# Two joins of a two-layer trunk on one core: when a norm's sums, its weights and the columns of a last step come

## The chip, the cores and the metric

The kernel runs on one core of a Trainium2 chip. The metric is the device time of one execution in microseconds; the time of a kernel is the median over its runs. TensorE (PE) multiplies, VectorE (DVE), ScalarE (ACT) and GpSimd (POOL) do elementwise work, SyncE (SP) issues the loads. TensorE's clock has two levels, 2.4 and 1.2 GHz; the profile shows the granted one as a share of the full one.

## The reference

Two layers over 512 latent columns and 256 context columns, each of 1024 features in float32. Layer 0 mixes with an mLSTM, layer 1 with windowed attention to latent and context keys; each is followed by an MLP.

```python
def _rms_norm(x, g):
    xf = x.astype(F32)
    y = xf * lax.rsqrt(jnp.mean(xf * xf, axis=-1, keepdims=True) + NORM_EPS)
    return (y * g.astype(F32)).astype(x.dtype)
...
def _modulate(x, shift, scale):
    return x * (1.0 + scale) + shift
...
def _sq_relu_mlp(u, w1, w2):
    return jnp.square(jax.nn.relu(u @ w1)) @ w2
```

Every mixer and every MLP reads `_modulate(_rms_norm(h), shift, scale)` and adds its result, times a gate, to `h`. What follows is about two places: from layer 0's output projection to its MLP, and from that MLP's last step to the keys of layer 1.

## The kernel before, in words

Features lie on partitions, in 8 tiles of 128 (index m or kt); columns lie along the free axis, latent (L, 512) and context (C, 256) apart. A float32 product is three matmuls (`mm3`, L96 to L98): high part times high, high times low, low times high. So every weight is split: `unit` loads a block of 512 KB (a DMA on SP into one of three raw buffers), ACT casts the high part (whi, L919), DVE subtracts to get the low one (wlo, L920), into one of four pairs of buffers. The order of instructions on each engine is made by a scheduler when the program is built, from the order of the code and from the buffers; it is fixed at run time. `feed` takes the next unit of a list, the plan, and puts it on the list `begun`; with `feed(True)` its cast and subtraction keep their place in the program.

A norm needs, for every column, the sum of squares over 8 tiles. `norm_add` (L302, L306) squares a tile on ACT and adds it to the tile ssC or ssL, on POOL; with `apart` the last two squares are not added but kept as tiles of their own (sq). Squares have two buffers, so one waits until the square two before it is used up. `norm_rc` then sums over partitions on TensorE: for every block of 128 columns one matmul against a column of ones for each kept tile (L319), below called ones-matmuls. DVE makes rs from it (L322), POOL raises it to the power -1/2 (rc, L324), TensorE turns rc into rows (L332, four transposes for L, two for C). Then DVE, ACT and DVE make u for each tile: t = h times both factors (L962 in the MLP, L341 in layer 1), the high part uH (or uC), and the low part uL.

**Join 1** is `out_late`. Products of heads 0 to 5 for the tiles 6 and 7 come first: (6,L), (6,C), (7,L), (7,C), 18 matmuls each. Then, for C and after it for L, each of the eight tiles gets the part of heads 6 and 7 (`wl`), DVE adds it to h (L508), and `norm_add` follows. `norm_hooks` gives two steps: the sums (`norm_rc`) and the whole norm. The C hooks run after the first two L tiles, the L hooks in `plain`, the MLP's first chunk, behind the C products of its tiles 0 and 1. `plain` takes four units of w1, C columns first.

```python
for g in "CL":
    for n, m in enumerate((6, 7, 0, 1, 2, 3, 4, 5)):
...
        self.norm_add(self.st, g, n, self.out_add(m, g, t), apart=n > 5)
```

**Join 2** is the last chunk (c = 7) of `ffn0` and `keys_begin`. There the columns are in two halves of 384: t = 0 is latent 0 to 383, t = 1 is latent 384 to 511 with all of C. `back` multiplies the hidden tiles (12 matmuls for each tile m and half) with units of w2 and adds to h (L1156). Tiles 0 to 3 are done for both halves, unit after unit, then tiles 4 to 7 for t = 1 and for t = 0. The C hooks run at tiles 4 and 5 of t = 0. `keys_begin` loads the four key units (wskv) and multiplies them with the context columns (96 matmuls, pj), with the L hooks after the first and the second half of the first block; the latent keys follow in `layer1_mix`, and their results go through rp, ksp and ks to the transposes of L1489.

## Time and profile before

| what | value |
|---|---|
| median of 3 runs (lowest, highest) | 1603.83 us (1600.60, 1606.53) |
| the profiled execution, its span | 1609.09 us, 1607.3 us |
| mean granted clock | 0.986 |
| PE, weight load of PE | 1552.3 us (97%), 1390.9 us (87%) |
| DVE, ACT, POOL | 1007.7 us (63%), 677.1 us (42%), 404.1 us (25%) |

The profile is one execution; its times count from the start of the span. Rows of a timeline give the start, the length, the engine, the line and operation, out<-in, the shape and how often, and in brackets the idle time just before and what ended it. A matmul's length covers its passage through the engine, so the distance of two starts tells what one costs; a ones-matmul is two records. A window's row gives its length and the busy time of PE, PE's weight load, DVE, ACT and POOL (with how many instructions), then the granted clock, the DMA engines' busy share and GB/s.

### The profile page before, as it was taken

The page shows a single profiled execution, that of the slowest core. Times are in us where ns is not written, and L with a number is a line of the kernel's source. Part 1 is how long each engine was busy: PE and PEld are TensorE (multiplying, and loading weights), DVE is VectorE, ACT ScalarE, POOL GpSimd, SP SyncE. Part 2 cuts the span into 40 slices and gives each one's busy share as a digit, 9 for nine tenths or more (in the row PEclk, how much of TensorE's full clock was granted, in tenths as well). Part 3 has the DMA queues.
Part 4 walks back from the last instruction along what each step waited for, and adds up shares of the span by engine and source line. Part 5 has one row for each costly group of instructions (what it writes and reads, how often), then busy time and mean ns, then how long its engine had stood idle before and what let it go on. Part 6 is the DMA issues. An engine that isn't in the chain of part 4 may idle for free.

```text
span 1607.3 us, 23962 instructions
## 1 busy us (share of the span) xinstructions
PE 1552.3 (97%) x9246; PEld 1390.9 (87%) x9246; DVE 1007.7 (63%) x1886; ACT 677.1 (42%) x1399; POOL 404.1 (25%) x378
## 2 busy tenths in 40 slices
PE   7989999999999999999999999989999999999997
PEld 4768888878899999999999998888887888888886
DVE  3665647478586888777667666767887533333333
ACT  4433333344473432433524445666675423233231
POOL 0221111113303221322232230454443302011122
PEclk9999999999999999999999999999999999999999
DMA  8322323134221343344344321010111322332221
GB/s 304 135 72 100 118 68 109 66 115 152 85 79 40 117 136 128 119 150 147 113 142 132 118 79 34 27 51 16 54 40 36 110 92 92 97 100 92 92 92 53
DMA packets 48857, 156.77 MB, mean 98 GB/s; under 512 B 5439, under 2 KB 11071, under 8 KB 48615
## 3 DMA queue, kind: packets, MB, share of 16 engines
q1 hardware_dynamic: 46992, 153.73, 29.2%
q8 instruction: 73, 1.20, 0.3%
q10 hardware_dynamic: 1751, 1.51, 0.3%
q14 instruction: 41, 0.34, 0.1%
HBM read 153.12 MB, written 2.10 MB: 97 GB/s over the span
## 4 chain that ended last, share of the span: by engine, by line
PE 72%; DVE 7%; issue 5%; POOL 5%; ACT 5%; DMA 1%; POOLq 0%; DVEq 0%; ACTq 0%
PE mm L97 17%; PE mm L96 17%; PE mm L98 17%; DVE adap L273 2%; PE p L97 2%; PE p L98 2%; PE p L96 2%; PE pt L1580 1%; PE pj L96 1%; PE pj L97 1%; PE pj L98 1%; PE at L836 1%; ACT whi L919 1%; DVE wlo L920 1%; PE av L1596 1%
## 5 line engine op out<-in xcount | busy, mean ns | idle before, releaser
L919 ACT CAST whi<-raw 128x1024 fp32r<-128x1024 f32 (+2 forms) x183 | 183.8, 1009 | 255.2 <-PE mm L97 208.7
L920 DVE TENSOR_TENSOR wlo<-raw,whi 128x1024 fp32r<-128x1024 f32 (+2 forms) x180 | 216.3, 1206 | 114.2 <-ACT whi L919 109.3
L96 PE MATMUL mm<-uH,whi 128*128 128x512 f32 (+1 forms) x488 | 188.8, 392 | 4.1 <-ACT v L702 4.0
L97 PE MATMUL mm<-uL,whi 128*128 128x512 f32 (+1 forms) x488 | 186.2, 384 | 0.3
L98 PE MATMUL mm<-uH,wlo 128*128 128x512 f32 (+1 forms) x488 | 185.4, 383 | 0.0
L273 DVE SCALAR_TENSOR_TENSOR adap<-raw,crow 128x1024 bf16<-128x1024 f32 x128 | 166.2, 1299 | 21.6 <-DMA raw<-ada 20.8
L96 PE MATMUL mm<-h,whi 128*128 128x384 f32 x512 | 173.2, 338 | 1.8 <-ACT h L919 1.8
L97 PE MATMUL mm<-h,whi 128*128 128x384 f32 x512 | 172.5, 337 | 0.5 <-DVE h L920 0.3
L98 PE MATMUL mm<-h,wlo 128*128 128x384 f32 x512 | 172.1, 336 | 0.0
L894 POOL TENSOR_TENSOR r<-r 128x512 f32<-128x512 f32 (+1 forms) x35 | 52.2, 1493 | 259.8 <-ACT r L893 259.8
L96 PEld LDWEIGHTS mm<-uH,whi 128*128 128x128 f32 x488 | 91.8, 190 | 20.5 <-ACT v L702 4.2
L97 PEld LDWEIGHTS mm<-uL,whi 128*128 128x128 f32 x488 | 92.2, 190 | 17.6 <-issue 1.2
L98 PEld LDWEIGHTS mm<-uH,wlo 128*128 128x128 f32 x488 | 91.9, 189 | 17.9 <-issue 0.3
L96 PE MATMUL mm<-hH,whi 128*128 128x512 f32 (+1 forms) x272 | 104.0, 382 | 0.0
L97 PE MATMUL mm<-hL,whi 128*128 128x512 f32 (+1 forms) x272 | 103.9, 382 | 0.0
L98 PE MATMUL mm<-hH,wlo 128*128 128x512 f32 (+1 forms) x272 | 103.8, 382 | 0.0
L919 ACT CAST whi<-sum 128x512 fp32r<-128x512 f32 (+1 forms) x42 | 31.9, 762 | 168.2 <-PE mm L97 77.8
L96 PEld LDWEIGHTS mm<-h,whi 128*128 128x128 f32 x512 | 96.1, 188 | 2.7 <-ACT h L919 2.7
L97 PEld LDWEIGHTS mm<-h,whi 128*128 128x128 f32 x512 | 96.2, 188 | 1.3 <-DVE h L920 1.2
L98 PEld LDWEIGHTS mm<-h,wlo 128*128 128x128 f32 x512 | 96.1, 188 | 0.0
L904 DVE SCALAR_TENSOR_TENSOR hL<-mm,mod,hL 128x512 f32<-128x512 f32 (+1 forms) x34 | 24.5, 720 | 102.7 <-PE mm L98 102.7
L98 PE MATMUL p<-t,wlo 128*128 128x384 f32 x224 | 75.4, 337 | 0.4 <-DVE wlo L920 0.4
(354 smaller groups left out, 4003.4 us busy)
## 6 DMA issues: line engine op xcount, KB each, us to landing
raw<-w SPq DMA_DIRECT2D x96, 512.0 KB, 3.4
raw<-ada SPq DMA_DIRECT2D x80, 512.0 KB, 3.5
raw<-w2a SPq DMA_DIRECT2D x32, 512.0 KB, 3.5
adaw<-ada SPq DMA_DIRECT2D x16, 512.0 KB, 6.8
hL<-xT SPq DMA_DIRECT2D x16, 256.0 KB, 4.1
raw<-wqk SPq DMA_DIRECT2D x8, 512.0 KB, 3.9
raw<-wv SPq DMA_DIRECT2D x8, 512.0 KB, 3.6
raw<-wo SPq DMA_DIRECT2D x8, 512.0 KB, 3.4
```

Source lines behind the costliest of these rows:

```text
L96: mm(out=out, lhsT=ah, rhs=bh, start=start, stop=False)
L97: mm(out=out, lhsT=ah, rhs=bl, start=False, stop=False)
L98: mm(out=out, lhsT=al, rhs=bh, start=False, stop=stop)
L273: self.tc.keep_in_program_order(nc.vector.scalar_tensor_tensor(out=pr, in0=w, scalar=0.5, in1=self.crow[:, v, :], op0=ALU.mult, op1=ALU.mu ...
L836: mm(out=o[hh][:, i * VW:(i + 1) * VW], lhsT=pw[g, d, hh][:, i, :], rhs=v[:, 3 * g + i, hh, :], start=False, stop=i == 2)
L894: nc.gpsimd.tensor_tensor(out=r, in0=r, in1=r, op=ALU.mult)
L904: nc.vector.scalar_tensor_tensor(out=h, in0=ps, scalar=self.mod[layer][:, 40 + m, v:v + 1], in1=h, op0=ALU.mult, op1=ALU.add)
L919: keep(self.nc.scalar.copy(out=hi, in_=src))
L920: keep((eng or self.nc.vector).tensor_tensor(out=lo, in0=src, in1=hi.bitcast(F32), op=ALU.subtract))
L1580: nc.tensor.transpose(out=pt[:, i * P:(i + 1) * P], in_=ps_[i][:, n * P:(n + 1) * P], identity=self.ident)
L1596: mm(out=o, lhsT=vv, rhs=pl, start=False, stop=n == len(blks) - 1)
```

## The change

At join 1 the last tile's first 18 latent matmuls move from ahead of the C part to behind it; the plan with w1 starts here, two units are fed early, and two, pinned, when the MLP begins; the last two squares are no longer apart but added on DVE (an argument that `norm_add` had). At join 2 `back` gets all four units of w2 at once: tiles 0 to 3 and then 4 to 7 of t = 1, then all eight of t = 0. The C hooks run at tiles 0 and 1 of t = 0. The key units end the plan and are fed behind the odd tiles of t = 0; the L hooks run behind the second and fourth tile pair of the keys' first half block.

```diff
--- before.py
+++ after.py
@@ -529,20 +529,28 @@
         xs = self.xs(yu)
         self.st = {}
         self.open_ff0()
-        ps, w = {}, {}
-        for m, g in ((6, "L"), (6, "C"), (7, "L"), (7, "C")):
-            if m not in w:
-                w[m] = self.unit(a["wout"][m, :, 0:6 * P])
-            n = NCX if g == "C" else NL
-            t = ps[m, g] = (self.mm if g == "L" else self.at).tile([P, 512], F32, name="mm", tag="mm" if g == "L" else "at")[:, :n]
+        ps = {}
+        w = {m: self.unit(a["wout"][m, :, 0:6 * P]) for m in (6, 7)}
+        self.begun, self.plan = [], [lambda m=m: self.unit(a["w1"][0, m]) for m in range(4)]
+
+        def begin(m, g):
+            pool, tag = (self.mm, "mm") if g == "L" else (self.at, "at")
+            t = ps[m, g] = pool.tile([P, 512], F32, name="mm", tag=tag)[:, :NCX if g == "C" else NL]
             for kt in range(6):
                 sl = slice(kt * P, (kt + 1) * P)
                 self.mm3(t, w[m][0][:, sl], w[m][1][:, sl], *xs[g](kt), kt == 0, False)
+        begin(6, "L")
+        begin(6, "C")
+        begin(7, "C")
         self.split_y0(yu, (6, 7))
         wl = [self.unit(a["wout"][4 * i:4 * i + 4, :, 6 * P:]) for i in (1, 0)][::-1]
+        self.feed()
         self.ada_until(0, 4)
         self.scale_vec(self.affn[0], 0, 4, 2)
         for g in "CL":
+            if g == "L":
+                begin(7, "L")
+                self.feed()
             for n, m in enumerate((6, 7, 0, 1, 2, 3, 4, 5)):
                 t = ps.get((m, g))
                 new = t is None
@@ -552,7 +560,7 @@
                 for i in range(2):
                     sl = slice((m % 4 * 2 + i) * P, (m % 4 * 2 + i + 1) * P)
                     self.mm3(t, wl[m // 4][0][:, sl], wl[m // 4][1][:, sl], *xs[g](6 + i), new and i == 0, i == 1)
-                self.norm_add(self.st, g, n, self.out_add(m, g, t), apart=n > 5)
+                self.norm_add(self.st, g, n, self.out_add(m, g, t), nc.vector if n > 5 else None)
                 if g == "L" and n < 2:
                     hooks[n]()
             hooks = self.norm_hooks(g)
@@ -1005,9 +1013,6 @@
         def unit_w2(c, i):
             return lambda: self.unit(a["w2a"][c, i])
 
-        def unit_w1(m):
-            return lambda: self.unit(a["w1"][0, m])
-
         def pair_w1(m0, m1):
 
             st = {}
@@ -1157,17 +1162,14 @@
                                                op0=ALU.mult, op1=ALU.add)
             if c == NC - 1:
                 g = "LC"[t]
-                self.norm_add(self.st, g, m, self.hview(g, m), apart=m > 5)
-        self.plan = []
+                self.norm_add(self.st, g, m, self.hview(g, m), nc.vector if m > 5 else None)
         for c in range(NC):
-            if c == 0:
-                self.plan += [unit_w1(m) for m in range(4)]
-            else:
+            if c:
                 self.plan += [f for i in range(2) for f in pair_w1(4 * c + i, 4 * c + 2 + i)]
             self.plan += [unit_w2(c, i) for i in range(4)]
-        self.begun = []
-        for _ in range(4):
-            self.feed()
+        self.plan += [lambda pr=pr, i=i: self.unit(a["wskv"][pr, i]) for pr in range(2) for i in range(2)]
+        for _ in range(2):
+            self.feed(True)
         for c in range(NC):
             hid = [[pair(f"h{t}", k) for t in range(2)] for k in range(4)]
             if c == 0:
@@ -1190,15 +1192,15 @@
                 continue
             pre()
             self.np = self.temps([f"t{n}{k}" for k in range(4) for n in "123b"])
-            for i in range(2):
-                w = self.begun.pop(0)
-                back(c, [(t, 2 * i + m) for t in (1, 0) for m in range(2)], hid, {i: w}, i == 0)
-            ws = {i: self.begun.pop(0) for i in (2, 3)}
-            for t in (1, 0):
-                for m in range(4, KT):
+            ws = {i: self.begun.pop(0) for i in range(4)}
+            back(c, [(1, m) for m in range(4)], hid, ws, True)
+            for t, ms in ((1, range(4, KT)), (0, range(KT))):
+                for m in ms:
                     back(c, [(t, m)], hid, ws)
-                    if t == 0 and m < 6:
-                        hooks[m - 4]()
+                    if t == 0 and m < 2:
+                        hooks[m]()
+                    if t == 0 and m % 2:
+                        self.feed()
                 hooks = done("LC"[t])
         return hooks
 
@@ -1228,15 +1230,16 @@
 
     def keys_begin(self, u, hooks):
 
-        self.wkv = [[self.unit(self.a["wskv"][pr, i]) for i in range(2)] for pr in range(2)]
+        w = self.begun
+        self.wkv = [w[:2], w[2:]]
         self.kvc = []
         for j in (4, 5):
             t = self.mm.tile([P, 512], F32, name="pj", tag="mm")
             for pr in range(2):
                 for i in range(4):
                     self.proj_part(self.wkv[pr], j, self.rows_of(u), 256, i, t[:, 256 * pr:256 * pr + 256])
-                if j == 4:
-                    hooks[pr]()
+                    if j == 4 and pr == 0 and i % 2:
+                        hooks[i // 2]()
             self.kvc.append(t)
 
     def layer1_mix(self, u):
```

TensorE, join 1, around the latent ones-matmuls; mm<-uC are the MLP's first context products. Before, cut behind the second group:

```order
L319 MATMUL at<-ones,ssL 128x1
L319 MATMUL at<-ones,sq 128x1
L96 MATMUL mm<-uC_4280,whi 128x256
L97 MATMUL mm<-uC_4280,whi 128x256
L98 MATMUL mm<-uC_4280,wlo 128x256
L96 MATMUL mm<-uC_4281,whi 128x256
L97 MATMUL mm<-uC_4281,whi 128x256
L98 MATMUL mm<-uC_4281,wlo 128x256
L96 MATMUL mm<-uC_4282,whi 128x256
L319 MATMUL at<-ones,sq 128x1
L319 MATMUL at<-ones,ssL 128x1
L319 MATMUL at<-ones,sq 128x1 x2
```

With the change:

```order
L96 MATMUL mm<-uC_4292,whi 128x256
L97 MATMUL mm<-uC_4292,whi 128x256
L319 MATMUL at<-ones,ssL 128x1 x4
L98 MATMUL mm<-uC_4292,wlo 128x256
L96 MATMUL mm<-uC_4293,whi 128x256
```

Twelve ones-matmuls in two groups have become four in one, with ssL alone as their source.

DVE, join 1, from the last latent update of h to the first latent u of the MLP (h1 is a split of a hidden tile). Before:

```order
L508 SCALAR_TENSOR_TENSOR hL5_3534<-mm_4373,mod0_81,hL5_3534 128x512
L920 TENSOR_TENSOR wlo_4398<-raw_4395,whi_4397 128x1024
L920 TENSOR_TENSOR wlo_4404<-raw_4401,whi_4403 128x1024
L920 TENSOR_TENSOR h1_4408<-r_4440,h1_4408 128x256
L322 TENSOR_SCALAR rs_4458<-at_4445 128x4
L962 SCALAR_TENSOR_TENSOR u320_4032<-hL0_3350,affn0_85,at_4508 128x512
```

With the change:

```order
L306 TENSOR_TENSOR ssL_4267<-ssL_4267,sq_4381 128x512
L306 TENSOR_TENSOR ssL_4267<-ssL_4267,sq_4392 128x512
L928 TENSOR_TENSOR wlo_4398<-raw_4395,whi_4397 128x1024
L928 TENSOR_TENSOR wlo_4404<-raw_4401,whi_4403 128x1024
L928 TENSOR_TENSOR h1_4408<-r_4440,h1_4408 128x256
L322 TENSOR_SCALAR rs_4450<-at_4445 128x4
L928 TENSOR_TENSOR h1_4410<-r_4479,h1_4410 128x256
L970 SCALAR_TENSOR_TENSOR u320_4032<-hL0_3350,affn0_85,at_4500 128x512
```

Two additions stand ahead of the two weight subtractions, and rs stands behind all of them.

DVE, join 2, from the last updates of h to the first latent tile of layer 1's norm (nt, uC: the context norm; the wlo are key units). Before:

```order
L1156 SCALAR_TENSOR_TENSOR hL7_4146<-mm_9338,mod0_81,hL7_4146 128x384
L343 SCALAR_TENSOR_TENSOR uC3_9013<-nt_9302,mod1_82,uC3_9013 128x256
L341 SCALAR_TENSOR_TENSOR nt_9306<-hC4_3524,amix1_84,at_9287 128x256
L341 SCALAR_TENSOR_TENSOR nt_9310<-hC5_3535,amix1_84,at_9287 128x256
L920 TENSOR_TENSOR wlo_9375<-raw_9372,whi_9374 128x1024
L343 SCALAR_TENSOR_TENSOR uC4_9014<-nt_9306,mod1_82,uC4_9014 128x256
L343 SCALAR_TENSOR_TENSOR uC5_9015<-nt_9310,mod1_82,uC5_9015 128x256
L341 SCALAR_TENSOR_TENSOR nt_9314<-hC6_4136,amix1_84,at_9287 128x256
L341 SCALAR_TENSOR_TENSOR nt_9318<-hC7_4147,amix1_84,at_9287 128x256
L322 TENSOR_SCALAR rs_9416<-at_9403 128x4
L343 SCALAR_TENSOR_TENSOR uC6_9016<-nt_9314,mod1_82,uC6_9016 128x256
L343 SCALAR_TENSOR_TENSOR uC7_9017<-nt_9318,mod1_82,uC7_9017 128x256
```

With the change:

```order
L1161 SCALAR_TENSOR_TENSOR hL4_3523<-mm_9290,mod0_81,hL4_3523 128x384
L343 SCALAR_TENSOR_TENSOR uC6_9008<-nt_9236,mod1_82,uC6_9008 128x256
L343 SCALAR_TENSOR_TENSOR uC7_9009<-nt_9240,mod1_82,uC7_9009 128x256
L1161 SCALAR_TENSOR_TENSOR hL5_3534<-mm_9307,mod0_81,hL5_3534 128x384
L928 TENSOR_TENSOR wlo_9327<-raw_9324,whi_9326 128x1024
L1161 SCALAR_TENSOR_TENSOR hL6_4116<-mm_9330,mod0_81,hL6_4116 128x384
L1161 SCALAR_TENSOR_TENSOR hL7_4127<-mm_9347,mod0_81,hL7_4127 128x384
L928 TENSOR_TENSOR wlo_9367<-raw_9364,whi_9366 128x1024
L306 TENSOR_TENSOR ssL_9183<-ssL_9183,sq_9344 128x512
L306 TENSOR_TENSOR ssL_9183<-ssL_9183,sq_9361 128x512
L322 TENSOR_SCALAR rs_9388<-at_9383 128x4
L341 SCALAR_TENSOR_TENSOR nt_9409<-hL0_3350,amix1_84,at_9404 128x512
```

The context norm's last tiles have moved ahead of the last three updates of h, two key units stand among these, and rs follows two additions.

## Rows read from the trace of the kernel before

**Rows 1.** page: busy us by engine; chain by engine; one DMA issue row

```profile
PE 1552.3 (97%) x9246; PEld 1390.9 (87%) x9246; DVE 1007.7 (63%) x1886; ACT 677.1 (42%) x1399; POOL 404.1 (25%) x378
...
PE 72%; DVE 7%; issue 5%; POOL 5%; ACT 5%; DMA 1%; POOLq 0%; DVEq 0%; ACTq 0%
...
raw<-w SPq DMA_DIRECT2D x96, 512.0 KB, 3.4
```

**Rows 2.** waits of TensorE, 420 to 440 us: in total, times, longest

```profile
PE at L319 <- POOL ssL L306: 3.7, 1, 3.7
```

**Rows 3.** windows: five engines' busy us, granted clock, DMA share, GB/s

```profile
434.30:438.00 3.70, 0.00 (x0) 0.00 (x0) 2.53 (x2) 0.92 (x4) 3.58 (x2) 1.00 0.48 149
438.00:440.00 2.00, 1.99 (x11) 2.00 (x12) 0.43 (x1) 1.33 (x3) 0.00 (x0) 0.63 0.68 248
440.00:445.00 5.00, 5.00 (x25) 5.00 (x24) 0.16 (x1) 0.00 (x0) 0.37 (x1) 0.50 0.00 2
445.00:450.00 5.00, 5.00 (x29) 5.00 (x29) 2.41 (x5) 2.57 (x5) 0.65 (x1) 0.63 0.02 5
955.00:960.00 5.00, 4.73 (x39) 4.35 (x38) 4.91 (x10) 3.72 (x7) 0.00 (x0) 1.00 0.19 77
960.00:965.00 5.00, 5.00 (x31) 5.00 (x32) 2.23 (x7) 0.91 (x2) 1.82 (x5) 0.66 0.32 108
1226.00:1235.00 9.00, 7.01 (x44) 6.60 (x44) 4.68 (x12) 4.05 (x11) 4.19 (x6) 0.81 0.01 2
```

**Rows 4.** TensorE by line, 434 to 453.2 us: busy us, mean ns

```profile
L97 PE MATMUL mm<-uC,whi 128*128 128x256 f32 x21 | 7.2, 341 | 0.0
```

**Rows 5.** tile ssL, 420 to 440 us: min, median, max ns

```profile
L306 POOL TENSOR_TENSOR ssL<-ssL,sq x5: 1296/1308/2124, 423.1 to 435.8; 128x512 f32<-128x512 f32 x5
```

**Rows 6.** timeline of DVE, join 1: start us, length us, instruction

```profile
412.38 1.22 DVE L920 TENSOR_TENSOR wlo<-raw,whi 128x1024 fp32r<-128x1024 f32 x1
...
430.64 2.72 DVE L508 SCALAR_TENSOR_TENSOR hL<-mm,mod,hL 128x512 f32<-128x512 f32 x4
433.28 3.55 DVE L920 TENSOR_TENSOR wlo<-raw,whi 128x1024 fp32r<-128x1024 f32 x2
...
447.59 0.75 DVE L962 SCALAR_TENSOR_TENSOR u<-hL,affn,at 128x512 f32<-128x512 f32 x1 [3.03 <-PE at L332]
...
459.18 0.74 DVE L965 SCALAR_TENSOR_TENSOR uL<-u,mod,uH 128x512 fp32r<-128x512 f32 x1
```

**Rows 7.** timeline of TensorE, join 1, end of the context part

```profile
453.00 0.28 PE L98 MATMUL mm<-uC,wlo 128*128 128x256 f32 x1
453.12 0.40 PE L96 MATMUL mm<-uH,whi 128*128 128x512 f32 x1
```

**Rows 8.** timeline of POOL, join 1, the power for rc

```profile
444.63 1.02 POOL L324 TENSOR_TENSOR rc<-rs,mhalf 128x4 f32<-128x4 f32 x1 [6.68 <-DVE rs L322]
```

**Rows 9.** timeline of TensorE, join 2

```profile
946.97 0.28 PE L319 MATMUL at<-ones,ssC 128*128 128x1 f32 x2
...
948.23 0.42 PE L96 MATMUL mm<-h,whi 128*128 128x384 f32 x1
...
954.82 0.28 PE L96 MATMUL pj<-whi,uC 128*128 128x256 f32 x1
...
971.74 0.28 PE L96 MATMUL pj<-whi,uH 128*128 128x256 f32 x1
```

**Rows 10.** waits of TensorE, 945 to 1000 us

```profile
PE pt L1489 <- DVE ksp L1482: 1.4, 2, 1.0
...
PE pj L96 <- ACT uC L342: 0.3, 1, 0.3
```

**Rows 11.** timeline of DVE, join 2

```profile
950.61 0.62 DVE L1156 SCALAR_TENSOR_TENSOR hL<-mm,mod,hL 128x384 f32<-128x384 f32 x1 [2.05 <-PE mm L98]
...
954.89 0.86 DVE L341 SCALAR_TENSOR_TENSOR nt<-hC,amix,at 128x256 f32<-128x256 f32 x2
...
968.36 1.41 DVE L341 SCALAR_TENSOR_TENSOR nt<-hL,amix,at 128x512 f32<-128x512 f32 x2 [6.01 <-PE at L332]
```


## The prediction

> **What bounds the kernel now.** I read the busy times and the chain first. TensorE is busy for 1552 of 1607 us, and the chain that ended last lies on it for 72% [rows 1]. A change that leaves its matmuls alone, as this one does, can gain only where TensorE stands still or runs at its lower clock. Then the waits and the table by windows, at the two places that the change touches.
>
> At the join from the output projection to the MLP ("join 1") the longest wait of TensorE in that part stands: 3.7 us for the sums of squares that POOL makes [rows 2]. The windows show what comes behind it: the granted clock is 1.00 before and through the wait, then 0.63, 0.50 and 0.63, that is the 1.2 GHz level (0.50) for about 1.5 + 5.0 + 3.7 = 10.2 us [rows 3]. TensorE does half as much there, so 5.1 us are lost. Check by the sum: from 434.3 to the first latent matmul of the MLP at 453.1 there are 18.8 us; the work in it is some 60 matmuls of 256 columns (21 of each of three kinds, less three that were running) at 0.12 us (7.2 us; [rows 4, 7]), 12 ones-matmuls at 0.21 us (2.5 us; six of them at the full clock take from 946.97 to 948.23 [rows 9]) and about 0.5 us of transposes. 10.2 + 3.7 + 5.1 = 19.0, close enough.
>
> At the join from the MLP to layer 1 ("join 2") there is no long wait. The context keys take from 954.82 to 971.74, 16.9 us [rows 9], for 96 matmuls at 0.12 us (11.5). The rest is 12 ones-matmuls (2.5), a 0.3 us wait [rows 10], transposes (0.5) and a half clock of 0.34 x 2 x 5 = 3.4 us, 1.7 lost; it begins among the ones-matmuls, in a stretch where TensorE was busy [rows 3]. Behind the latent keys stand 1.4 us of waits for DVE, whose latent norm started only at 968.36 [rows 10, 11].
>
> **Join 1, part by part.** (a) Sums. The table of the tile gives POOL's latent adds 1.30 us for the quickest, 1.31 for the median and 2.12 for the slowest, and the last starts at 435.8 [rows 5]; so it ends at 437.9, and the last four began near 431.0 (two slow, two quick). The slow two ran while DVE did two weight subtractions, 3.55 us for two against 1.22 alone [rows 6]. The change pins those two units behind the sums, so I take 1.30 four times. The C part also starts about 0.8 us earlier, since the 18 latent matmuls of the last tile leave its path and cover the C sums afterwards; POOL ends at about 430.2 + 5.2 = 435.4 where it ended at 437.9. If the adds stay at 2.12, it is 438.5.
> (b) New: the last two squares are added by DVE, one behind the other, and the first waits for POOL's last add, which also frees the last square's buffer. The trace has no 128x512 add of squares on DVE; the nearest rows are a 128x512 update at 0.68 and a two-input uL of 0.74 [rows 6]; the outer bound is POOL's 2.12. I take 0.7, so 1.4 for both: ones from 436.8, a wait of 2.4 us instead of 3.7. At 2.12 each it would be 439.6.
> (c) Four ones-matmuls for twelve: 0.85 instead of 2.5, 1.7 gained.
> (d) The pinned units: two subtractions of 1.22 and one hidden-tile split of 0.4 stand on DVE ahead of rs, so rs comes at 436.7 + 2.9 = 439.6 and rc, 1.02 us on POOL [rows 8], at 440.7. TensorE has 22 C matmuls (2.6 us) from 437.6 to 440.3 to cover it; 0.4 to 0.5 us are left as a new wait.
> (e) After it 0.5 us of transposes and 30 C matmuls (3.6): the latent part starts at 444.8 at full clock.
> (f) Clock. Half level after a 2.4 us wait: I take one short spell, 3.4 us, as between 1226 and 1235, where TensorE stood still for 2.0 of 9 us (0.19 x 2 x 9 us [rows 3]); it loses 1.7. Bounds: none, and 10.2 us as now.
> Latent start 446.5 against 453.1, 6.6 earlier. DVE's first latent u comes at about 441.6 against 447.59, 6.0 earlier, and its eight tiles take until 459.9 now [rows 6]; what follows can't lead by much more than this. **Gain 6.0**; 7.4 without any half clock, 4.3 with 6.8 us of it, 2.5 with 10.2.
> Moved weight loads: SyncE's order of loads is unchanged and the bytes are the same; during the wait the DMA engines are busy for 0.48 [rows 3], so I cost them at nothing; without that cover a unit would come later by the time of its landing, 3.4 us [rows 1], and the first plain product with it. The 18 moved matmuls cost nothing, as they run in a place where TensorE had only the wait for the C norm.
>
> **Join 2.** Let t0 be the end of the MLP's last matmul (954.82 before). (g) Ones C fall from six to two: 0.85 gained ahead of t0. (h) The context norm is made four products earlier, its last tile is ready some 2 us before t0, and the 0.3 us wait goes. (i) The key weights: all four casts and subtractions now lie in the last eight products, where two did, and the last cast waits for the buffers of the last product. DVE's work from the C transposes on is 16 updates of 256 columns at 0.43 at least, 4 subtractions at 1.22 and 7 updates of 384 at 0.62, 16.1 us [rows 6, 11], against seven products of 12 matmuls, 14.6 us by the 36 that take from 948.23 to 954.82 with two transposes among them [rows 9], so DVE ends late: the last weight half at t0 + 2.6, the two new adds at t0 + 4.0. TensorE has 34 key matmuls (4.05) to cover exactly that. (j) Ones L: 0.87 instead of 2.5; then three matmuls, rs and rc (1.2): a new wait of 1.2 us, transposes end at t0 + 7.1. (k) 58 key matmuls, 6.9: latent keys start at t0 + 14.0 against 16.9. (l) DVE's latent norm starts at t0 + 7 against 13.5, so the 1.4 us waits behind the keys [rows 10] go. Sum 0.85 + 2.9 + 1.4 = 5.2; a half-clock spell of 3.4 us, which I keep since a wait and ones-matmuls still come together, was in before's 16.9 and not in the 14.0: 5.2 - 1.7 = 3.5. **Gain 3.5**; bounds 5.2 without that spell and 1.3 (the third rival).
>
> Here a rule of the Trainium skill speaks against the change: "SBUF — State Buffer", section "Who interferes with whom", says that a DVE instruction with two SBUF inputs and a POOL instruction that reads SBUF share a port and exclude each other. The 2.12 against 1.30 agrees. By it the extra weight subtractions of (i) would collide with POOL's latent sums and the whole sum would be 7.3 instead of 9.5; the third rival works this out from rows.
>
> **Sum.** 6.0 + 3.5 = 9.5 us. The profiled execution took 1609.1 (span 1607.3), 5.3 above the median of 1603.8, so its own counterpart is 1599.6; on the median **1594.3 us**. Half a percent, 8 us, is about what can be told from no change.
>
> **Rivals.**
> 1. No half clock at either join. For it: TensorE's stretches of ones are a third as long. Against: the waits at 434 and at 1229 each have one behind them [rows 3], and at 960 it came with hardly a wait. 7.4 + 5.2 = 12.6: 1591.2.
> 2. Half clock at join 1 as long as before, and the waits behind the keys stay, because DVE is full there. For it: the 10.2 us, and DVE's 4.91 of 5 us at 955 [rows 3]. Against: the wait ahead of it shrinks, and DVE's latent norm starts earlier. 2.5 + (0.85 + 2.9 - 1.7) = 4.6: 1599.2.
> 3. Port contention at join 2: four subtractions beside POOL's sums instead of two. Each costs DVE 0.56 more (3.55 / 2 - 1.22) [rows 6], so the ones come 2.2 later, past the 34 matmuls of cover. Against: POOL has at most five adds there, in 14.6 us. 9.5 - 2.2 = 7.3: 1596.5. The rule of the Trainium skill's page "SBUF — State Buffer" cited above says the same.
> 4. Slower: the chain POOL, square, DVE add, weight halves, rs, rc becomes the bound at both joins. If all adds run at 2.12 and the halves at 1.78, POOL ends at 438.6, the ones come at 442.8, rs 4.0 later, and the transposes end at 448.3: latent start 451.9 at full clock, 457.0 with 10.2 us at half, 3.9 us lost. At join 2 the same makes the ones 3.3 later (t0 + 7.5); 14.0 + 3.3 and 3.4 for 6.8 us at half give t0 + 20.7, 3.0 lost net of the 0.85. Then 1610.7. It decides once the sums come about 5 us later at each join than I reckon. Against it: no subtraction is left beside POOL's adds at join 1.
> 5. The change doesn't do what it says: the order would have to be undone at run time, and engines run theirs in order. 1604.
>
> **How the numbers follow.** Forecast 0.40, rival 1 0.15, rival 2 0.20, rival 3 0.16, rival 4 0.06, rival 5 0.03. Gains above 8 us: rival 1, the larger part of the forecast (0.30) and the near edge of rival 3 (0.05): 0.50. Slower by over 8 us: rival 4 with its upper half, and a little for what I don't see, 0.05. The rest, 0.45, within 0.5%. The range takes in rivals 1 to 3 with some 2.7 us on either side, 1588.5 to 1602.0; rivals 4 and 5 and the tails lie outside, some 0.15.
>
> **What would show it.** TensorE's wait for the sums at join 1 down to 2 to 3 us, with the DVE add as its releaser; POOL's four latent adds all near 1.30; 0.63, 0.50, 0.63 replaced by one window below 1.00; the first latent matmul of the MLP 6 us earlier; the wait of 1.0 us for ksp gone. Wrong if the adds stay at 2.12, if the half clock lasts over 7 us, or if TensorE waits over 2 us for ones at join 2.

## The result, and the profile after

The changed kernel takes **1593.58 us** (median of 4 runs, 1590.88 to 1593.87), the kernel before 1602.89 in the 4 runs of the same comparison: 9.3 us less, ratio 0.9936 with a 95% interval of 0.9914 to 0.9958. The forecast was 1594.3, its range 1588.5 to 1602.0; of its chances the 0.50 on "faster by over half a percent" came true. The profiled execution took 1593.31 us, its span is 1591.5.

The sum came out right with both of its terms wrong, so the two places are read one by one. The page first: busy times by engine.

```profile
PE 1538.4 (97%) x9198; PEld 1378.8 (87%) x9198; DVE 1013.9 (64%) x1894; ACT 676.2 (42%) x1399; POOL 402.2 (25%) x378
```

TensorE has 48 records fewer than in [rows 1]: at each join 8 ones-matmuls for the latent columns and 4 for the context ones, two records each. DVE has eight instructions more, the last two squares of C and of L at both joins.

Timeline of TensorE, nine starts that mark the places: the first product of `out_late`, the ones-matmuls and the rows of join 1, the MLP's first latent matmul; the last matmul of the MLP's first layer (pb), the last product of its second layer with the wait ahead of it; first context keys, first latent keys, first scores.

```profile
395.12 0.47 PE L96 MATMUL mm<-uH,whi 128*128 128x512 f32 x1
...
432.61 1.02 PE L319 MATMUL at<-ones,ssL 128*128 128x1 f32 x8 [1.82 <-DVE ssL L306]
...
437.58 0.60 PE L332 MATMUL at<-ident,rc 128*128 128x128 f32 x4
...
441.73 0.40 PE L96 MATMUL mm<-uH,whi 128*128 128x512 f32 x1
...
907.33 0.33 PE L98 MATMUL pb<-tb,wlo 128*128 128x384 f32 x1
...
942.66 0.69 PE L96 MATMUL mm<-h,whi 128*128 128x384 f32 x1 [2.23 <-DVE hL L1161]
946.31 0.28 PE L96 MATMUL pj<-whi,uC 128*128 128x256 f32 x1
...
960.11 0.28 PE L96 MATMUL pj<-whi,uH 128*128 128x256 f32 x1
...
983.51 0.58 PE L1537 MATMUL s<-ks,qs 128*128 128x256 f32 x1 [0.78 <-DVE qs L1512]
```

The same marks of before, in the timeline of its TensorE (its first latent matmul is in [rows 7], its first keys in [rows 9]):

```profile
398.45 0.47 PE L96 MATMUL mm<-uH,whi 128*128 128x512 f32 x1
...
918.82 0.33 PE L98 MATMUL pb<-tb,wlo 128*128 128x384 f32 x1
...
997.19 0.38 PE L1534 MATMUL s<-ks,qs 128*128 128x256 f32 x1 [0.68 <-ACT qs L1509]
```

Distances of such starts are what I compare from here on. **J1** is from the first product of `out_late` to the MLP's first latent matmul, **J2** from the start of the MLP's last first-layer matmul (pb) to the first scores:

| stretch, us | before | after | gain |
|---|---|---|---|
| J1 | 54.67 | 46.61 | 8.1 |
| J2 | 78.37 | 76.18 | 2.2 |
| of J2: to the first context key | 36.00 | 38.98 | -3.0 |
| context keys | 16.92 | 13.80 | 3.1 |
| latent keys, to the scores | 25.45 | 23.40 | 2.1 |

The two profiled executions lie 15.8 us apart. 3.3 of these lie ahead of J1 (398.45 against 395.12), where both run the same code, and some 2 behind J2; so the time of one execution says less than its stretches. The stretch between J1 and J2 hardly changed, 465.70 us before and 465.60 after. 8.1 + 2.2 = 10.3 us stand against the 9.3 us of the medians.

The waits of TensorE from 420 to 1000 us (in total, times, longest), the four that bear on the joins:

```profile
PE mm L96 <- DVE hL L1161: 2.2, 1, 2.2
PE at L319 <- DVE ssL L306: 1.8, 1, 1.8
...
PE at L332 <- POOL rc L324: 0.8, 1, 0.8
...
PE pt L1492 <- DVE ksp L1485: 0.3, 1, 0.3
```

The 3.7 us of [rows 2] are 1.8 now, with the DVE addition as the releaser, and the 1.4 us behind the keys [rows 10] are 0.3. New are 0.8 for rc at join 2 and, the longest of all, 2.2 us for an update of h. The windows around both waits (columns as in [rows 3]):

```profile
428.00:432.00 4.00, 2.79 (x24) 2.58 (x22) 1.59 (x4) 2.56 (x5) 2.78 (x3) 1.00 0.00 0
432.00:437.00 5.00, 4.39 (x26) 4.42 (x27) 3.74 (x6) 3.20 (x7) 1.02 (x1) 0.68 0.43 125
437.00:442.00 5.00, 5.00 (x42) 4.96 (x42) 3.78 (x6) 3.00 (x6) 0.00 (x0) 0.97 0.27 92
926.00:936.00 10.00, 10.00 (x61) 9.96 (x61) 7.33 (x14) 4.59 (x9) 2.91 (x2) 1.00 0.17 54
936.00:946.00 10.00, 7.78 (x37) 7.45 (x36) 9.91 (x15) 5.43 (x11) 5.89 (x4) 0.83 0.16 52
```

At join 1 the half level (0.50) lasts 0.32 x 2 x 5 + 0.03 x 2 x 5 = 3.5 us, 3.4 by windows of 1 us, where it lasted 10.2. At join 2 DVE is busy for 9.91 of 10 us ahead of the keys, TensorE for 7.78, and a spell of 0.17 x 2 x 10 = 3.4 us lies here, no longer among the ones-matmuls.

### The profile page after: what moved, and what is told of

Read it like the earlier page. It is cut to its first block, busy times and chain, and to the rows that moved or that the text cites. A ratio compares the mean times of both kernels' runs of the same rounds, so it can differ in the third digit from the quotient of the medians.

```text
span 1591.5 us, 23868 instructions
## 1 busy us (share of the span) xinstructions
PE 1538.4 (97%) x9198; PEld 1378.8 (87%) x9198; DVE 1013.9 (64%) x1894; ACT 676.2 (42%) x1399; POOL 402.2 (25%) x378
## 4 chain that ended last, share of the span: by engine, by line
PE 71%; DVE 8%; issue 5%; POOL 5%; ACT 4%; DMA 1%; POOLq 0%; DVEq 0%; ACTq 0%
PE mm L97 17%; PE mm L96 17%; PE mm L98 17%; DVE adap L273 2%; PE p L98 2%; PE p L97 2%; PE p L96 2%; PE pt L1583 1%; PE pj L96 1%; PE pj L98 1%; PE pj L97 1%; DVE wlo L928 1%; PE at L844 1%; ACT whi L927 1%; PE av L1599 1%
```

## The experiments

Each starts from the changed kernel; its diff is against that. Where the comparison with the kernel before had three or more rounds, the ratio is given; the kernel before had medians from 1601.41 to 1602.35 us in these comparisons, so ratios compare better than times.

**Each join by itself.** `j1_alone` has join 2 as before the change (step order of `back`, hooks, key units loaded in `keys_begin`, squares apart); `j2_alone` has join 1 as before.

```diff
 j1_alone
-                self.norm_add(self.st, g, m, self.hview(g, m), nc.vector if m > 5 else None)
+                self.norm_add(self.st, g, m, self.hview(g, m), apart=m > 5)
-        self.plan += [lambda pr=pr, i=i: self.unit(a["wskv"][pr, i]) for pr in range(2) for i in range(2)]
...
 j2_alone
-                self.norm_add(self.st, g, n, self.out_add(m, g, t), nc.vector if n > 5 else None)
+                self.norm_add(self.st, g, n, self.out_add(m, g, t), apart=n > 5)
-            self.feed(True)
...
+            self.feed()
...
```

> Join 1 as changed, join 2 as before. Reading of the two traces: the stretch from the last tile's first products to the first latent matmul of the MLP shrank by 8.2 us, so about 8 us less than before in all (ratio about 0.995), the wait for the sums near 1.8 us behind a DVE add, one spell of half clock of 3.4 us, and the MLP's lead kept until join 2. By the split of the prediction it would be 6.0 us (0.9963). If the gain came from elsewhere in the program, under 3 us.

> Join 2 as changed, join 1 as before. Reading of the traces: 2 to 3 us less than before (ratio about 0.9985): a new wait of about 2.2 us of TensorE for DVE inside the last eight products, with half clock behind it, takes back most of some 5 us that the keys gain. By the split of the prediction 3.5 us. If the new wait is an effect of join 1 (DVE later there), it is missing here and the gain is 5 us or more.

`j1_alone`: 1595.28 us, ratio 0.9959 (0.9944 to 0.9975), J1 46.67, a gain of 8.0. `j2_alone`: 1602.24 us, ratio 0.9998 (0.9985 to 1.001), J2 76.28, a gain of 2.1, with the same wait of 2.2 us for h. By the stretches the joins are independent: 8.0 + 2.1 against 8.1 + 2.2 together. Join 1 is worth more than the 6.0 forecast, join 2 less than the 3.5, and its wait doesn't come from DVE being late since join 1. The whole times can't decide this: the medians give 6.1 us for join 1, whose interval holds 6.0 as well as 8.0, and nothing clear of zero for join 2.

**Join 1, one part undone at a time.** First the pinned units, then the squares, then the moved products:

```diff
 w1_unpinned
-            self.feed(True)
+            self.feed()
 squares_apart_j1
-                self.norm_add(self.st, g, n, self.out_add(m, g, t), nc.vector if n > 5 else None)
+                self.norm_add(self.st, g, n, self.out_add(m, g, t), apart=n > 5)
 tile7_ahead
         begin(6, "C")
+        begin(7, "L")
         begin(7, "C")
...
             if g == "L":
-                begin(7, "L")
                 self.feed()
```

> The change, but the two w1 units at join 1 are not pinned behind the sums: their casts and subtractions may move up among the last squares. If it is the port shared by DVE and POOL that made two of POOL's adds take 2.12 us, they take 2.12 again here, the wait of TensorE for the sums goes from 1.8 to 3 us or more, and the stretch from the late products to the first latent product of the MLP (46.6 us in the change, 54.7 before) takes 48 to 52. If the pin does nothing, 46.6.

> The change, but at join 1 the last two squares stay apart, so the ones-matmuls are 12 and 6 again and DVE adds nothing. If the number of ones-matmuls is worth what it costs on TensorE alone, the stretch of 46.6 us becomes 48.5 (8 matmuls at 0.21) less some 0.8 for the two DVE adds that go. If the run of ones-matmuls also holds the clock down, as the 10.2 us at half in the kernel before suggest, it becomes 50 us or more with over 6 us at half clock.

> The change, but the 18 latent matmuls of the last tile stand ahead of the context part again. If they cover the context norm in the change, TensorE waits for rc of the context norm here and the context u come up to 4 us later relative to the latent updates, so that the sums come later: the stretch of 46.6 us becomes 48 to 50. If the place does not matter, 46.6 within 0.3.

| | J1, us | lost against the change | half level at join 1, us |
|---|---|---|---|
| before | 54.67 | 8.1 | 10.2 |
| change | 46.61 | | 3.4 |
| `w1_unpinned` | 48.99 | 2.4 | 6.8 |
| `squares_apart_j1` | 51.03 | 4.4 | 6.8 |
| `tile7_ahead` | 49.82 | 3.2 | 6.8 |

(One execution each, of 1593.55, 1593.83 and 1595.21 us; the gains read from J1.) In `w1_unpinned` both weight subtractions get in among the sums again: one beside POOL's adds, the other between DVE's two additions. The table of the tile ssL, join 1 (min, median, max ns), rows of DVE's timeline, and the wait of TensorE:

```profile
L306 POOL TENSOR_TENSOR ssL<-ssL,sq x5: 1292/1302/2159, 416.2 to 428.9; 128x512 f32<-128x512 f32 x5
```

```profile
430.27 0.69 DVE L306 TENSOR_TENSOR ssL<-ssL,sq 128x512 f32<-128x512 f32 x1 [2.57 <-POOL ssL L306]
430.88 1.22 DVE L928 TENSOR_TENSOR wlo<-raw,whi 128x1024 fp32r<-128x1024 f32 x1
432.01 0.69 DVE L306 TENSOR_TENSOR ssL<-ssL,sq 128x512 f32<-128x512 f32 x1
```

```profile
PE at L319 <- DVE ssL L306: 2.3, 1, 2.3
```

In the change POOL's three last adds took 4.04 us together, 1.35 each; here one took 2.16, near the slow ones of [rows 5], and the second subtraction holds up DVE's second addition. The ones come 2.4 us later in the stretch, the wait is 0.5 longer, since 16 more context matmuls lie ahead of it. In `tile7_ahead` the ones of C wait too, having lost the 18 matmuls that covered them, and so does TensorE for rc (waits of TensorE, 405 to 445 us, then POOL's timeline):

```profile
PE at L319 <- DVE ssL L306: 2.1, 1, 2.1
PE at L332 <- POOL rc L324: 0.8, 1, 0.8
PE at L319 <- DVE ssC L306: 0.4, 1, 0.4
```

```profile
435.71 1.94 POOL L324 TENSOR_TENSOR rc<-rs,mhalf 128x4 f32<-128x4 f32 x1 [3.37 <-DVE rs L322]
```

rc took 1.94 us instead of 1.02 [rows 8], and as long in `squares_apart_j1`: in both, the two subtractions stand behind rs on DVE and run beside POOL's power, where in the change they stand ahead of rs.

`squares_apart_j1` keeps POOL's adds quick and waits 2.2 us, yet loses most: it has twelve ones-matmuls, eight more at the 0.21 us of the forecast, and the granted clock is down in two windows:

```profile
433.00:438.00 5.00, 5.00 (x27) 5.00 (x26) 2.44 (x3) 0.75 (x4) 1.94 (x1) 0.53 0.18 48
438.00:443.00 5.00, 5.00 (x37) 5.00 (x36) 3.49 (x6) 2.55 (x7) 0.00 (x0) 0.79 0.47 169
```

The losses add up to 10.0, more than the 8.1 gained: 3.4 us more at half level, 1.7 lost, lie in each of the three. So the parts are no independent sums; in these executions all three were needed to have the short spell. Without its price the losses are 0.7, 2.7 and 1.5 us, 4.9 in all; with the 3.4 us that 6.8 us less at half level give back, this makes 8.3 for the 8.1.

**Join 2: why TensorE waits for h.** Products take PSUM buffers from a pool of three in turn, so a product waits for the DVE update of the one three before it. `bank_alternate` gives every second product of t = 0 a buffer from the other pool:

```diff
-                        pool, tag = (self.at, "at") if len(pss) % 2 else (self.mm, "mm")
+                        pool, tag = (self.at, "at") if (len(pss) if len(todo) > 1 else t == 0 and m) % 2 else (self.mm, "mm")
```

> The change, but the eight products of the first half in the last step take their PSUM banks from both pools in turn, so that a product needs not wait for the update of h three products earlier. If the banks are what costs, the wait of 2.2 us and the half clock behind it (1.7) go and the kernel is 3 to 4 us faster than the change. If DVE is behind with its work whatever TensorE does, the wait moves to the latent ones-matmuls (some 3 us there instead of none) and the time is that of the change within 1 us.

1590.89 us, ratio 0.9928 (0.9907 to 0.9949; the interval overlaps that of the change), but J2 is 76.17, as in the change. The wait for h is gone and comes back at the ones (timeline of TensorE, and the window around it):

```profile
949.00 1.87 PE L319 MATMUL at<-ones,ssL 128*128 128x1 f32 x8 [2.06 <-DVE ssL L306]
```

```profile
946.00:956.00 10.00, 7.66 (x39) 7.16 (x39) 5.50 (x9) 2.51 (x4) 2.28 (x6) 0.66 0.32 105
```

The half level lasts 0.34 x 2 x 10 = 6.8 us here for the 3.4 of the change, so that J2 is the same to 0.01 is in part chance: 1.7 us of it are a longer spell. The wait itself is nearly as long as before (2.06 for 2.23), so the buffers choose its place. DVE is behind. `keys_late` and `keys_half` take work off it ahead of the keys: all four key units, or the second pair, are loaded in `keys_begin` as before the change.

```diff
 keys_late
-        self.plan += [lambda pr=pr, i=i: self.unit(a["wskv"][pr, i]) for pr in range(2) for i in range(2)]
...
-        w = self.begun
-        self.wkv = [w[:2], w[2:]]
+        self.wkv = [[self.unit(self.a["wskv"][pr, i]) for i in range(2)] for pr in range(2)]
 keys_half
...
+        self.wkv = [self.begun[:2], [self.unit(self.a["wskv"][1, i]) for i in range(2)]]
```

> The change, but the four key units are loaded when the keys begin, as before, and not in the plan. If the four casts and subtractions among the last eight products are what puts DVE behind, the wait of 2.2 us falls under 0.7 and the last product ends 2 to 4 us earlier; the keys may then wait for their own weights up to 2 us, so 0 to 3 us faster than the change. If POOL's sums alone slow DVE, the wait stays near 2 us and the time is within 1 us of the change or slower.

> The change, but only the first two key units are in the plan; the other two are loaded when the keys begin. If DVE's load among the last eight products is what decides join 2, the stretch from the last low product of the MLP to the first scores (78.4 us before, 76.2 in the change, 72.9 with all four late) lies between, at 72 to 75. If the weights' lateness at the keys matters more than DVE's load, it is shorter than 72.9; the wait of 2.2 us for the update of h tells: under 1 us.

`keys_late`: J2 72.88, 3.3 better, with no half level in it, which is 1.7 of the 3.3; 1593.58 us, ratio 0.9936 (0.9911 to 0.9961). That is the change's median: four runs from 1587.52 to 1595.59 don't show the 3.3. The wait for h is gone (a window over J2, and waits, 900 to 960 us):

```profile
914.00:987.00 73.00, 69.45 (x490) 67.92 (x488) 55.18 (x124) 39.82 (x87) 17.02 (x22) 1.00 0.20 67
```

```profile
PE at L319 <- DVE ssL L306: 1.2, 1, 1.2
PE pj L97 <- DVE wlo L928: 0.7, 1, 0.7
```

`keys_half` is a miss: J2 77.07 where I expected a value between 72 and 75; 1593.25 us, ratio 0.9938 (0.9917 to 0.9958). The same view:

```profile
PE mm L96 <- DVE hL L1161: 2.2, 1, 2.2
PE at L319 <- DVE ssL L306: 1.1, 1, 1.1
```

Half the load is removed, and the wait for h is as long as before. The pair that I had left ahead is the one that stands on DVE in front of the awaited update; DVE's order is fixed, so the place counts and not the total. DVE around the wait, in the timeline of the changed kernel:

```profile
937.65 1.82 DVE L928 TENSOR_TENSOR wlo<-raw,whi 128x1024 fp32r<-128x1024 f32 x1
939.40 1.90 DVE L343 SCALAR_TENSOR_TENSOR uC<-nt,mod,uC 128x256 fp32r<-128x256 f32 x2
941.22 0.86 DVE L341 SCALAR_TENSOR_TENSOR nt<-hC,amix,at 128x256 f32<-128x256 f32 x2
942.00 0.60 DVE L1161 SCALAR_TENSOR_TENSOR hL<-mm,mod,hL 128x384 f32<-128x384 f32 x1
```

A subtraction of 1.82 us and a pair of low parts of 1.90 stand ahead of the update. Alone they take 1.22 and, by the next run, 0.88. Meanwhile POOL's sums are slow too (table of the tile ssL, 925 to 952 us):

```profile
L306 POOL TENSOR_TENSOR ssL<-ssL,sq x5: 1287/2147/2203, 931.3 to 944.8; 128x512 f32<-128x512 f32 x5
```

`sums_on_dve_j2` gives these five adds to DVE: more work for the late engine, none beside it.

```diff
-                self.norm_add(self.st, g, m, self.hview(g, m), nc.vector if m > 5 else None)
+                self.norm_add(self.st, g, m, self.hview(g, m), nc.vector if m > 5 or g == "L" else None)
```

> The change, but at join 2 DVE makes all seven latent additions of squares and POOL none. If what puts DVE behind is POOL holding the shared port, the pairs of uC near 1.9 us and the key units near 1.8 to 2.0 us fall to 0.95 and 1.22, and the wait of 2.2 us for the update of h shrinks although DVE has 3.5 us more to do. If DVE is slow there for its own load, the wait grows to 3 us or more and the pairs stay near 1.9.

J2 is 72.94, 3.2 better (one execution, 1587.69 us). DVE's timeline, the same two kinds of instruction as above, and a window:

```profile
931.84 0.88 DVE L343 SCALAR_TENSOR_TENSOR uC<-nt,mod,uC 128x256 fp32r<-128x256 f32 x2
...
940.15 1.21 DVE L928 TENSOR_TENSOR wlo<-raw,whi 128x1024 fp32r<-128x1024 f32 x1
```

```profile
940.00:960.00 20.00, 18.95 (x145) 18.56 (x146) 16.42 (x25) 8.20 (x13) 1.80 (x5) 1.00 0.23 79
```

The waits for h are two now, 1.6 us in all, and the clock is full from 940 to 960, so 1.7 of the 3.2 us are the spell and the rest is DVE. Five more adds (0.68 each, 3.4 us) left DVE's busy time of the whole kernel where it was, 1013.6 against 1013.9: what it no longer loses to POOL pays for them.

**Toward a better version.** `keys_late_three_sums` is `keys_late` with a third square of L added by DVE at join 1; `keys_late_four_sums` takes a fourth and sets the L hooks of the keys later; `all_five` joins three sums at join 1, all on DVE at join 2, alternating buffers, and one key unit early, the second pair of keys pinned between the hooks.

```diff
 keys_late_three_sums
-                self.norm_add(self.st, g, n, self.out_add(m, g, t), nc.vector if n > 5 else None)
+                self.norm_add(self.st, g, n, self.out_add(m, g, t), nc.vector if n > (4 if g == "L" else 5) else None)
 keys_late_four_sums
+                self.norm_add(self.st, g, n, self.out_add(m, g, t), nc.vector if n > (3 if g == "L" else 5) else None)
+                    if j == 4 and (pr, i) in ((0, 3), (1, 1)):
 all_five
+        self.plan += [lambda: self.unit(a["wskv"][0, 0])]
+                    if j == 4 and pr == 0 and i == 1:
+                        self.pin = True
+                        self.wkv.append([self.unit(self.a["wskv"][1, k]) for k in range(2)])
...
```

> The change with the key units loaded when the keys begin and, at join 1, the last three latent squares added by DVE instead of the last two. Join 2's stretch stays at 72.9 us (3.3 less than the change). At join 1 POOL ends one add (1.3 us) earlier and DVE adds 0.69: the wait of 1.8 us goes to about 1.1 and the stretch of 46.6 to about 46. In all 3.5 to 4 us faster than the change, ratio to the kernel before about 0.991. If only DVE's chain counts and the start of the latent part is bound elsewhere, join 1 stays at 46.6.

> As the last one, with the last four squares added by DVE and the steps of the latent norm of layer 1 two tile pairs later in the program. Join 1: if POOL's chain is what the ones-matmuls wait for, 45.5 us; if DVE's own order is (the first of its additions now stands ahead of the last update of h), 46.6 or more. Join 2 as in the last one.

> The change with five things altered that the runs so far priced: three latent squares added by DVE at join 1 (45.6 us for 46.6 there); at join 2 all latent squares added by DVE, the last eight products in banks of both pools, one key unit in the plan, the second when the keys begin, the other two pinned behind rs, in the time in which DVE waits for the transposes. If DVE's chain up to rs is what decides join 2 and POOL's hold on the port what makes it long, its stretch falls below the 72.9 us of either half measure, to 70 to 72, the wait for the update of h goes, and the kernel is 4 to 7 us faster than the change (ratio to the kernel before about 0.989). If PE waits for the two late key units instead, 73 us or more and some 4 us faster than the change at most.

| | us | ratio to before (95%) | J1 | J2 |
|---|---|---|---|---|
| change | 1593.58 | 0.9936 (0.9914 to 0.9958) | 46.61 | 76.18 |
| `keys_late_three_sums` | 1590.81 | 0.9924 (0.9906 to 0.9943) | 45.61 | 74.27 |
| `keys_late_four_sums` | 1587.74, one execution | | 45.88 | 74.33 |
| `all_five` | 1589.32 | 0.9918 (0.9900 to 0.9937) | 46.22 | 75.14 |

At join 1 a third sum shortens the wait for the ones from 1.8 to 1.1 us, and no window there is below full clock; 0.7 of the gain goes into a wait for rc (waits of `keys_late_three_sums`, 405 to 445 us, then of `keys_late_four_sums`, 425 to 446 us).

```profile
PE at L319 <- DVE ssL L306: 1.1, 1, 1.1
PE at L332 <- POOL rc L324: 0.7, 1, 0.7
```

```profile
PE mm L96 <- ACT whi L927: 0.6, 1, 0.6
```

The fourth removes the wait for the ones, and still brings nothing more, since a spell of 3.4 us is there again. At join 2 their code is that of `keys_late` (the second sets the L hooks later); both have a spell of 3.4 us there, and their J2 is 1.4 us longer. So later key units are worth 1.9 us with the spell and 3.3 without, and this change doesn't decide whether it comes. `all_five` misses its J2 of 70 to 72: the pinned pair of subtractions fell on the power that makes rc (timelines of DVE and of POOL, and the wait of TensorE, 900 to 975 us).

```profile
948.05 2.35 DVE L928 TENSOR_TENSOR wlo<-raw,whi 128x1024 fp32r<-128x1024 f32 x2
```

```profile
948.22 1.92 POOL L324 TENSOR_TENSOR rc<-rs,mhalf 128x4 f32<-128x4 f32 x1 [19.97 <-DVE rs L322]
```

```profile
PE at L332 <- POOL rc L324: 1.7, 1, 1.7
```

rc took 1.92 us, where it takes 1.02 [rows 8]. `all_five` has the lowest median of the kernels with several runs, and it beats the kernel before. It lies 4.3 us below the change, 2.9 by the ratios (0.9918 for 0.9936); but the two intervals overlap, so that it beats the change isn't shown by the times.

## Why the prediction was right or wrong

The profiled executions of before and after are laid on each other by the first product of `out_late`; a time of after on before's clock is its own plus 3.33.

**Join 1: mechanism right, size short (8.1 for 6.0).** Step by step:

- (a) held and was cautious. POOL's last add ended at 430.94, that is 434.3 where I had 435.4: three adds from 426.90 on took 4.04 us, and the one ahead of them lay 1.5 us before these, where I had all four in a row. That the pin keeps them quick is shown by `w1_unpinned`.
- (b) held: the two additions took 1.49 us together, the wait is 1.8 where I had 2.4, the ones start at 435.9 for 436.8.
- (c) held: 8 records instead of 24.
- (d) failed, to the good: there is no wait for rc. The C matmuls that cover it, 21 in the trace, ran mostly at half level, from the ones at 432.61 to the rows at 437.58, and rc was ready at 435.73 + 1.02 = 436.75. In `keys_late_three_sums`, where no half level came, the wait is there, with 0.7 us.
- (e), (f) held: one spell of 3.4 us; the latent part starts at 445.06, where I had 446.5. The 1.4 are the 0.9 of the ones and the 0.4 to 0.5 of rc.
- **The step that failed** is the cap, "what follows can't lead by much more than this": the 6.0 us by which DVE's first latent u leads. That u came at 441.55, forecast 441.6, but it doesn't bound TensorE. What can hold it is the last low part and the matmul that reads it first. DVE's last uL in the timelines, after:

```profile
448.35 1.41 DVE L973 SCALAR_TENSOR_TENSOR uL<-u,mod,uH 128x512 fp32r<-128x512 f32 x2
```

It is ready at 449.76, 11.5 us after the first u; before it took 12.3 (447.59 to 459.92, [rows 6]), with two splits of hidden tiles among them for one now. Of TensorE's latent matmuls the first to read it is the 38th now, the 33rd before, because the built order mixes a second product in earlier. It starts in after at 450.34, in before at 460.40:

```profile
450.34 0.39 PE L97 MATMUL mm<-uL,whi 128*128 128x512 f32 x1
```

```profile
460.40 0.39 PE L97 MATMUL mm<-uL,whi 128*128 128x512 f32 x1
```

That is 8.6 us behind the first latent matmul instead of 7.3, and 0.6 behind the low part, where it was 0.5. So TensorE may lead by 6.0 (first u) + 0.8 (shorter row of tiles) + 1.3 (later reader) - 0.1 (slack) = 8.0, the 8.1 measured. So 6.0 was no cap: with the 0.6 us left behind the low part it would be some 8.6 here. This is reckoned from the two executions; no run shows TensorE held there. I had read the order of DVE for it and not that of TensorE, and held the length of DVE's eight tiles fixed. `j1_alone` repeats the 8.0.

**Join 2: the sum too large (2.2 for 3.5), in one step.**

- (g), (j), (k), (l) held: the ones of C are fewer, a wait for rc came, of 0.8 us (I had 1.2), the latent keys started at t0 + 13.8 (14.0), and the stretch behind them is 2.1 shorter (1.4). The ones of L came at t0 + 4.06, as (i) had it.
- **The step that failed is in (i)**: "DVE ends late" was right, but I let the whole lateness fall behind t0, under the 34 key matmuls. DVE works without a pause from 929.78 to 947, and TensorE needs it before t0: every product takes a PSUM buffer that an update of h must empty. Ahead of the last product it stood 2.2 us for the update three products earlier, that of tile 4, and a 3.4 us spell at half level came behind it. So t0 came 3.0 us later in J2: 2.2 + 1.7 - 0.85 for the fewer ones of C. I had it 0.85 earlier, and 0.85 later with the 1.7 us of the spell that I kept among the ones and that was spent here. `bank_alternate` shows that lateness and not buffers is the cause, `keys_half` and `keys_late` that it is the work in front of that one update. That the spell belongs to this wait isn't shown: in `keys_half` and `squares_apart_j1` the same wait of 2.2 us stands at the same place, but the spell came 10 us later, among the keys, and t0 only 1.5 us late.
- The price of DVE's work was a lower bound in (i): 0.43 for an update of 256 columns, 1.22 for a subtraction. From 932.23 on the pairs of low parts took 1.91 and 1.90 where 0.87 is free, one subtraction 1.82: 1.04 + 1.03 + 0.60 = 2.7 us more ahead of the update that TensorE waited 2.2 for. That is the port contention of the third rival, in another place than it had it. Its price of 2.2 us was about right by luck: it priced four subtractions at 0.56, and what stood in front of the update were two pairs of low parts and one slow subtraction. `sums_on_dve_j2` shows the contention by taking POOL's adds away.

The rule of the Trainium skill, "SBUF — State Buffer", section "Who interferes with whom", that a two-input DVE instruction and a POOL instruction that reads SBUF exclude each other at a shared port, agrees with the slow and quick lengths set side by side here, such as the pair of low parts at 1.90 beside POOL's adds and at 0.88 without them. I had weighed it for the four subtractions alone; the low parts (L343), which read two tiles as well, pay it too.

**The sum.** Join 1 gave 2.1 more and join 2 1.3 less, so 0.8 of error remained in the stretches. The medians lie 9.3 apart for the 9.5 forecast; that the forecast time missed by 0.7 comes from its starting point, 1603.8, where the kernel before had 1602.89 in this comparison. The hit of the total is partly luck: the two errors have no common cause. Of the rivals, 1, 2, 4 and 5 didn't happen; the third did, at about its price, and join 1's surplus hid it in the time.

What stays open: which activity of TensorE decides on a spell. At join 1 waits of 3.7, 2.1 to 2.3 and 1.8 us went with 10.2, 6.8 and 3.4 us, but 1.1 us went with none in `keys_late_three_sums` and with a spell of about 3.4 in `all_five`.

## What to carry to other kernels

Before moving elementwise work ahead of a join, ask for each awaited result what now stands in front of it on its in-order engine; a buffer pool of three made lateness felt ahead of the last product, for an update three products before it, and so sooner than at the join. Price DVE work beside POOL's additions by its slow rows, and if DVE is the late engine, try giving it these additions: here that was more work, done sooner, in one execution. And read a change of half a percent from stretches between fixed instructions: J1 lies between 46.59 and 46.67 us in the six executions that have the changed join 1, while whole executions of one kernel differ by 3 to 10 us. A spell at half clock that falls in, out or elsewhere still shifts a stretch: J2 of the changed join 2 is 76.18 to 76.32 in four executions and 76.96 in `squares_apart_j1`.

## What the runs showed of the hardware

- The contention holds in both directions and for tiny instructions: POOL's add of 128x512 took 2.15 to 2.20 us instead of 1.30, DVE's subtraction 1.82 to 2.00 instead of 1.22, a pair of low parts 1.90 instead of 0.88, and POOL's power on 128x4, four numbers for each partition, 1.92 to 1.94 in three runs, beside DVE's subtractions, instead of 1.02.
- A half-clock spell of 3.4 us came in `keys_late_four_sums` with no wait over 0.6 us at join 1, where there are also ones-matmuls; a shorter wait alone doesn't keep the clock up.
